# Fused MLP second projection of a two-layer decoder: weight sums by accumulating transfers, with the signs of the seven products turned

## The chip, the cores and the metric

The kernel runs on one core of one Trainium2 chip. The metric is the device time of one execution in microseconds (us). The kernel before takes 1547.85 us (median of 3 runs, 1546.98 to 1550.19).

## The reference: what is computed

Two decoder layers on 512 tokens of width 1024, all in fp32. Each layer has a token mixer, a cross-attention and an MLP, each between two RMS norms. The change lies in the MLP, whose part of the reference is:

```
hdn = jnp.square(jax.nn.relu(rms_norm(x, pre_mlp_g[l]) @ w_up[l]))      # 512 x 4096
x = x + rms_norm(hdn @ w_down[l], post_mlp_g[l])                        # w_down: 4096 x 1024
```

After layer 0's MLP comes the input projection of layer 1's mixer (`w_in`); after layer 1's MLP the result is written out.

## The kernel before, in words

**Products.** An fp32 product is made of three matmuls on halves of the operands: every operand is split into a rounded high part and a rest (`whi`, `wlo` of a weight, `fh`, `fl` of an activation), and `mm` (L239, L240, L241) issues wlo·fh, whi·fl and whi·fh. TensorE (PE) does these. ScalarE (ACT) makes the high part with a copy (L164 for a weight, L201 for an activation), VectorE (DVE) the rest with a subtraction (L165, L203).

**Weights.** `raw_w` (L157) loads a 512 KB tile of weights (128 partitions x 1024 fp32) on SP's queue into one of 8 `raw` buffers; `parts_w` makes `whi` and `wlo` from it, which have 5 buffers each.

**The MLP.** The 4096 hidden features are taken in four chunks of 1024 (`qd_` = 0 to 3), a chunk in two groups g of 512. Per group, an up projection (PE, tiles `pfm`) is evicted by ACT (L1067 relu, L1068 square) into `ra` and `rb`; then `left_forms` makes the seven left operands out of the four quarters a11, a21 (of `ra`) and a12, a22 (of `rb`). After both groups, the second projection is done with seven products in place of eight: p = 1 to 7, each a sum of quarters of the hidden values times a sum of quarters of `w_down`. The four quarters of the weights of each group, b11, b12, b21, b22, are loaded into four `raw` tiles (`B`), and `right_form` turns them into the sum that product p needs by subtractions on DVE, 128 x 1024 each, in place (L1033, L1035, L1037, L1039), before `parts_w`. A product is 24 matmuls of 512 columns (two groups, two row tiles i, two token tiles j, three each). Its result in PSUM (`wa`, `wc`, `we`) is added into the accumulators `acc` in SBUF by DVE (L1105 for the first, L1107 for the others). In chunks 0 to 2 the products come in the order 1, 5, 6, 2, 7, 3, 4; in the last chunk of a layer in the order 1, 2, 5, 6, 3, 7, 4, so that token tiles finish one after the other; `done` then weighs each half by the gain (L1045), `add_post_norm` computes the norm (a power on GpSimd, POOL, L139) and adds to `xs` (L423), and in layer 0 `norm_x` makes the next layer's normed input `xn` on POOL (L408), which PE transposes (L224, `tp`).

**The order of the work.** The program is written in dependency order and a scheduler lays the instructions of each engine in a row; each engine then runs its row in order, and waits where an operand or a buffer isn't ready. POOL has no transfers before the change: its row holds the norms' powers, the `xn` and softmax work.

The program text of the functions that the change touches:

Of the kernel before, what the change touches and what calls it, by code (L numbers as in the profile page):

```python
# [16 lines left out]
OP = mybir.AluOpType  # L17
# [28 lines left out]
def block_kernel(ctx: ExitStack, tc, x, mem, positions, rel_bias, w_in, q_norm_g, w_uq, kv_norm_g,  # L46
# [3 lines left out]
    nc = tc.nc  # L50
# [13 lines left out]
    def unit(name, shape=(128, 512), dt=F32):  # L64
        return un.tile(list(shape), dt, tag="u", name=name)

    def small(name, w):
        return sm.tile([128, 4], F32, tag="sm", name=name)[:, :w]

    def mm_ps(name):  # L70
        return psm.tile([128, 512], F32, tag="mm", name=name)
# [79 lines left out]
    def raw_w(src, r0, kts, c0, width):  # L151
        raw = wp.tile([128, 2, 512], F32, tag="raw", name="raw", bufs=8)

        first = {3: 1, 4: 3}.get(loads[1])
        loads[1] += 1
        with nullcontext() if first is None else tc.issue_after(x_loads[first]):
            loads[2] = nc.sync.dma_start(raw[:, :kts, :width], src[r0:r0 + kts * 128, c0:c0 + width].rearrange(  # L157
                "(k p) c -> p k c", p=128)).ins
        return raw

    def parts_w(raw):
        hi = wp.tile([128, 2, 512], WD, tag="hi", name="whi")
        lo = wp.tile([128, 2, 512], WD, tag="lo", name="wlo")
        nc.scalar.activation(hi, raw, AF.Copy)  # L164
        nc.vector.tensor_sub(lo, raw, hi.bitcast(F32))  # L165
        return hi, lo
# [33 lines left out]
    def split_from(hi, lo, src):  # L200
        token_parts[:] = [nc.scalar.activation(hi, src, AF.Copy).ins]  # L201
        if SPLIT:
            nc.vector.tensor_sub(lo, src, hi.bitcast(F32))  # L203
# [10 lines left out]
    def flush():  # L214
        while late and late[0][0] <= clk[0]:
            late.pop(0)[2]()
# [149 lines left out]
    def feat_major(*a, **k):  # L366
        run(feat_major_steps(*a, **k))
# [44 lines left out]
    def new_xt():  # L412
        h = xtp.tile([128, NK, S], WD, tag="xt", name="xth")
        l = xtp.tile([128, NK, S], WD, tag="xt", name="xtl") if SPLIT else None
        return h, l
# [11 lines left out]
    def row_bcast(src, l):  # L427
        gb = [unit("gb") for _ in range(2)]
        for n in range(2):
            nc.sync.dma_start(gb[n], bass.AP(tensor=src.tensor, offset=src.offset + l * D + n * 512,  # L430
                                               ap=[[0, 128], [1, 512]]))
        return gb
# [129 lines left out]
    for l in range(DEPTH):  # L562
# [434 lines left out]

        acc = [[None, None] for _ in range(NT)]  # L1000
        ss = [small("mss", 2) for _ in range(NT)]
        nxh = nxl = None
# [2 lines left out]
        def left_forms(F, ra, rb):  # L1005

            a11, a21 = ra[:, :, 0:256], ra[:, :, 256:512]
            a12, a22 = rb[:, :, 0:256], rb[:, :, 256:512]

            def part(p, src):  # L1010
                h, lo = unit("fh", (128, 2, 256), WD), unit("fl", (128, 2, 256), WD)
                split_from(h, lo, src)
                F[p].append((h, lo))

            s1, s2 = unit("s1", (128, 2, 256)), unit("s2", (128, 2, 256))
            part(1, a11)
            nc.vector.tensor_add(s1, a21, a22)
            part(5, s1)
            nc.vector.tensor_sub(s2, s1, a11)
            part(6, s2)  # L1020
            part(2, a12)
            nc.vector.tensor_sub(a21, a11, a21)
            part(7, a21)
            nc.vector.tensor_sub(a12, a12, s2)
            part(3, a12)
            part(4, a22)

        def right_form(p, b):


            b11, b12, b21, b22 = b
            if p == 5:
                nc.vector.tensor_sub(b11, b12, b11)  # L1033
            elif p == 6:
                nc.vector.tensor_sub(b11, b22, b11)  # L1035
            elif p == 7:
                nc.vector.tensor_sub(b12, b22, b12)  # L1037
            elif p == 4:
                nc.vector.tensor_sub(b11, b21, b11)  # L1039
            return parts_w({1: b11, 5: b11, 6: b11, 2: b21, 7: b12, 3: b22, 4: b11}[p])  # L1040

        def done(t, n):

# [12 lines left out]
        for qd_ in range(4):  # L1056
            if qd_ == 3 and l < DEPTH - 1:
                nxh, nxl = new_xt()
            F = {p: [] for p in range(1, 8)}
            for g in range(2):  # L1060
                ra = pp.tile([128, 1280], F32, tag="P", name="ra", bufs=2)[:, 0:1024]
                rb = pp.tile([128, 1280], F32, tag="PT", name="rb", bufs=2)[:, 0:1024]
                ra, rb = [r.rearrange("p (k c) -> p k c", k=2) for r in (ra, rb)]

                def ev_up(m, ps, ra=ra, rb=rb):
                    r = (ra, rb)[m // 2][:, m % 2, :]
                    nc.scalar.activation(r, ps, AF.Relu)  # L1067
                    nc.scalar.activation(r, r, AF.Square)  # L1068

                feat_major(w_up[l], (qd_ * 2 + g) * 512, 4, NK, G_MLP + 8 * l, xh_f, xl_f, S, ev_up,  # L1070
                           whole=2 if qd_ == 0 and g == 0 else 0)
                left_forms(F, ra, rb)
            B = [[raw_w(w_down[l], qd_ * 1024 + g * 512 + r * 256, 2, n * 512, 512)
                  for r in range(2) for n in range(2)] for g in range(2)]
            A = [pss.tile([128, 512], F32, tag="s", name="wa") for _ in range(2)]
            C = [pst.tile([128, 512], F32, tag="t", name="wc") for _ in range(2)]
            E = [None] * 2
            end = qd_ == 3


            plan = ((1, A, True, False, ((0, 0),)), (5, C, True, False, ((2, 1),)),
                    (6, A, False, False, ((0, 1),)), (2, E, True, True, ((0, 0),)),
                    (7, A, False, False, ((2, 1),)), (3, C, False, True, ((0, 1),)),
                    (4, A, False, True, ((2, 0),)))
            if end:
                plan = ((1, A, True, False, ((0, 0),)), (2, E, True, True, ((0, 0),)),
                        (5, C, True, False, ((2, 1),)), (6, A, False, False, ((0, 1),)),
                        (3, C, False, True, ((0, 1),)), (7, A, False, True, ((2, 1), (2, 0))),
                        (4, E, True, True, ((2, 0),)))
            for p, ps, first, last, dsts in plan:  # L1090
                if ps is E:
                    E[:] = [mm_ps("we") for _ in range(2)]

                def product(g, i, j, w):
                    c = slice(j * 128, (j + 1) * 128)
                    fh, fl = F[p][g]
                    mm(ps[j], fh[:, i, c], fl[:, i, c], w[0][:, i, :], w[1][:, i, :],
                       first and g + i == 0, g + i == 2, not first)

                def finish(j):  # L1100
                    for d, n in dsts:
                        t = d + j
                        if acc[t][n] is None:
                            acc[t][n] = unit("acc")
                            nc.vector.tensor_copy(acc[t][n], ps[j])  # L1105
                        else:
                            nc.vector.tensor_add(acc[t][n], ps[j], acc[t][n])  # L1107
                        if end and p in (2, 3, 4) or end and p == 7 and n == 1:
                            done(t, n)

                if end and p == 4:
                    for j in range(2):
                        for g in range(2):
                            for i in range(2):
                                product(g, i, j, last_w[g])
                        finish(j)
                        flush()
                    continue
                for g in range(2):
                    w = right_form(p, B[g])  # L1120
                    for i in range(2):
                        for j in range(2):
                            product(g, i, j, w)
                if end and p == 7:
                    last_w = [right_form(4, B[g]) for g in range(2)]
                if end and p == 1:
                    gb = row_bcast(post_mlp_g, l)
                for j in range(2):
                    finish(j)
                if end and p in (2, 5):  # L1130
                    for t in ((0, 1) if p == 2 else (2, 3)):
                        load_x(t, xmid)
                flush()
# [37 lines left out]
```

## Time and profile before

| | before |
|---|---|
| median of 3 runs | 1547.85 us |
| the profiled execution | 1551.81 us |
| span of its instructions | 1550.0 us |
| PE busy | 1509.1 us (97%) |
| DVE busy | 995.9 us (64%) |
| ACT busy | 820.0 us (53%) |
| POOL busy | 239.0 us (15%) |
| transfers | 164.09 MB, 106 GB/s on the mean |

Of the profiled execution's 1551.81 us, 1.81 lie around the span; it stands 3.96 us (0.26%) above the median. A timeline row gives a start, a duration, the engine, the program's line and the tiles; a bracket at its end says how long the engine stood idle before it and what ended the idle time. Busy times of matmuls overlap, so their pace is read from the distance of their starts.

### The profile page before, as it was taken

Reading aid. Unit: us, or ns where it says so; the run is one execution under the profiler, and the core shown is the slowest. Engines: PE = TensorE matmul, PEld = TensorE weight load, DVE = VectorE, ACT = ScalarE, POOL = GpSimd, SP = SyncE. Lnnn points to the kernel's source line nnn. Section 1 sums busy time; section 2 is a strip of 40 time slices with the busy share of each in tenths; the row PEclk is TensorE's granted clock in tenths of the full one; section 3 lists DMA queues with packets and bytes.
Section 4 is the critical chain, followed back from the end, with each engine's and each line's share of the span. In section 5 each row is a group of like instructions: output and inputs, shape, how many; then the busy total and the mean of one; then the engine's idle time right before and its main releaser. Section 6 shows DMA issues by size and latency. Waiting matters only on the chain.

```text
span 1550.0 us, 21290 instructions
## 1 busy us (share of the span) xinstructions
PE 1509.1 (97%) x7861; PEld 1265.6 (82%) x7861; DVE 995.9 (64%) x1780; ACT 820.0 (53%) x1578; POOL 239.0 (15%) x429
## 2 busy tenths in 40 slices
PE   8999999999999999999989999999999999999996
PEld 7777788898898888888868877978988988888885
DVE  5555775456458668585974667664654594958678
ACT  5355666346346464545554566653553654646363
POOL 2133631021020000000011355201111100000000
PEclk9989999999999999999999999999999999999999
DMA  6432223613131505151541322244322324060612
GB/s 235 143 116 69 79 65 109 204 55 119 53 114 50 181 28 177 41 166 59 179 131 51 122 81 91 69 140 145 109 82 68 115 71 155 17 195 20 190 55 82
DMA packets 87404, 164.09 MB, mean 106 GB/s; under 512 B 6230, under 2 KB 12036, under 8 KB 87300
## 3 DMA queue, kind: packets, MB, share of 16 engines
q1 hardware_dynamic: 86724, 161.68, 32.4%
q8 instruction: 62, 1.02, 0.3%
q10 hardware_dynamic: 576, 1.05, 0.2%
q14 instruction: 42, 0.34, 0.1%
HBM read 154.29 MB, written 11.03 MB: 107 GB/s over the span
## 4 chain that ended last, share of the span: by engine, by line
PE 84%; DVE 7%; issue 3%; ACT 2%; DMA 2%; POOL 1%; SPq 0%; DVEq 0%; POOLq 0%; ACTq 0%
PE pfm L240 12%; PE pfm L239 12%; PE pfm L241 12%; PE ptm L239 6%; PE ptm L240 6%; PE ptm L241 6%; PE wa L239 3%; PE wa L240 3%; PE wa L241 3%; PE sp L467 3%; PE op L230 3%; DVE wlo L197 2%; PE ptp L224 2%; PE wc L240 2%; PE wc L239 2%
## 5 line engine op out<-in xcount | busy, mean ns | idle before, releaser
L240 PE MATMUL pfm<-xth,wlo 128*128 128x512 f32 (+1 forms) x896 | 322.4, 360 | 0.6
L239 PE MATMUL pfm<-xtl,whi 128*128 128x512 f32 (+1 forms) x896 | 322.2, 360 | 0.0
L241 PE MATMUL pfm<-xth,whi 128*128 128x512 f32 (+1 forms) x896 | 321.6, 359 | 0.0
L197 DVE SCALAR_TENSOR_TENSOR wlo<-raw,gT,whi 128x512 fp32r<-128x512 f32 (+3 forms) x332 | 229.1, 729 | 131.6 <-ACT whi L192 129.9
L192 ACT ACTIVATE whi<-raw,gT 128x512 fp32r<-128x512 f32 (+2 forms) x324 | 209.2, 697 | 180.3 <-PE pfm L241 87.3
L164 ACT ACTIVATE whi<-raw 128x1024 fp32r<-128x1024 f32 x112 | 118.1, 1060 | 142.9 <-PE pfm L241 52.8
L240 PEld LDWEIGHTS pfm<-xth,wlo 128*128 128x128 f32 x896 | 169.2, 189 | 26.8 <-DVE wlo L197 1.4
L241 PEld LDWEIGHTS pfm<-xth,whi 128*128 128x128 f32 x896 | 169.2, 189 | 25.6 <-issue 0.5
L239 PEld LDWEIGHTS pfm<-xtl,whi 128*128 128x128 f32 x896 | 169.2, 189 | 24.8
L165 DVE TENSOR_TENSOR wlo<-raw,whi 128x1024 fp32r<-128x1024 f32 x112 | 134.8, 1217 | 34.3 <-ACT whi L164 34.3
L139 POOL TENSOR_TENSOR pnr<-pnm,mhalf 128x1 f32<-128x1 f32 x24 | 18.0, 750 | 828.8 <-DVE pnm L420 828.8
L475 POOL TENSOR_SCALAR P<-P,rs 128x128 f32<-128x128 f32 (+3 forms) x128 | 71.5, 563 | 151.6 <-DVE rs L474 81.2
L239 PE MATMUL wa<-wlo,fh 128*128 128x512 f32 x240 | 93.6, 390 | 0.5 <-DVE acc L1105 0.5
L241 PE MATMUL wa<-whi,fh 128*128 128x512 f32 x240 | 93.4, 389 | 0.0
L240 PE MATMUL wa<-whi,fl 128*128 128x512 f32 x240 | 93.4, 389 | 0.0
L473 ACT ACTIVATE P<-P,nm 128x128 f32<-128x128 f32 (+3 forms) x128 | 71.2, 557 | 34.1 <-DVE nm L471 33.4
L185 DVE TENSOR_TENSOR wlo<-raw,whi 128x1024 fp32r<-128x1024 f32 x32 | 39.1, 1222 | 59.3 <-ACT whi L184 58.6
L239 PE MATMUL ptm<-wlo,xth 128*128 128x512 f32 (+2 forms) x192 | 68.6, 359 | 3.4 <-DVE wlo L197 2.5
L184 ACT ACTIVATE whi<-raw 128x1024 fp32r<-128x1024 f32 x32 | 33.9, 1061 | 67.3 <-PE ptm L241 60.2
L240 PE MATMUL ptm<-whi,xtl 128*128 128x512 f32 (+2 forms) x192 | 67.1, 349 | 0.6 <-DVE xtl L203 0.6
L241 PE MATMUL ptm<-whi,xth 128*128 128x512 f32 (+2 forms) x192 | 66.3, 346 | 0.0
L224 PE MATMUL ptp<-ident,P 128*128 128x128 f32 x320 | 50.5, 282 | 3.9 <-ACT PT L494 2.3
(249 smaller groups left out, 3280.4 us busy)
## 6 DMA issues: line engine op xcount, KB each, us to landing
raw<-in_w_up SPq DMA_DIRECT2D x64, 512.0 KB, 4.6
raw<-in_w_down SPq DMA_DIRECT2D x64, 512.0 KB, 4.3
raw<-in_w_in SPq DMA_DIRECT2D x24, 512.0 KB, 5.5
raw<-in_w_xk SPq DMA_DIRECT2D x16, 512.0 KB, 5.4
raw<-in_w_xv SPq DMA_DIRECT2D x16, 512.0 KB, 3.6
raw<-in_w_mix_out SPq DMA_DIRECT2D x16, 512.0 KB, 4.7
raw<-in_w_xq SPq DMA_DIRECT2D x16, 512.0 KB, 6.4
raw<-in_w_xo SPq DMA_DIRECT2D x16, 512.0 KB, 4.1
```

Source lines behind the costliest of these rows:

```text
L164: nc.scalar.activation(hi, raw, AF.Copy)
L165: nc.vector.tensor_sub(lo, raw, hi.bitcast(F32))
L192: weight_parts[:] = [nc.scalar.activation(cols(hi, k, False), cols(raw, k, True), AF.Copy, scale=g).ins]
L197: nc.vector.scalar_tensor_tensor(lv, rv, g, hv, op0=OP.mult, op1=OP.subtract)
L224: ins = nc.tensor.transpose(out_, in_, ident_)
L230: nc.tensor.matmul(ps, lhsT=lhsT, rhs=rhs, start=start, stop=stop)
L239: nc.tensor.matmul(ps, lhsT=lh, rhs=rl, start=first, stop=False, skip_group_check=more)
L240: nc.tensor.matmul(ps, lhsT=ll, rhs=rh, start=False, stop=False, skip_group_check=more)
L241: nc.tensor.matmul(ps, lhsT=lh, rhs=rh, start=False, stop=last, skip_group_check=more)
L467: nc.tensor.matmul(sp[:, :L], lhsT=q[:, i * 128:(i + 1) * 128], rhs=k[:, :L], start=n == 0, stop=n == len(parts) - 1)
L473: nc.scalar.activation(Pi, Pi, AF.Exp, bias=nm[:, i:i + 1], scale=-1.0, accum_out=rs[:, i:i + 1])
L475: nc.gpsimd.tensor_scalar(Pi, Pi, rs[:, i:i + 1], 1.0, op0=OP.mult, op1=OP.mult)
```

## The change

Three things change in the MLP of both layers.

1. The sums of weights are made by a transfer: `right_form` no longer subtracts on DVE, but issues on POOL a `dma_start` with `accum_op=add` that reads another quarter of `w_down` from HBM (512 KB) and adds it into the `raw` tile that is to become the sum. There are 8 of these per chunk (products 5, 6, 7 and 4, two groups), 64 in all. b11 becomes b11+b12 for product 5, then b11+b12+b22 for 6, then that plus b21 for 4; b12 becomes b12+b22 for 7.
2. So that all sums are plain, signs move to the left operands (two `tensor_sub` become `scalar_tensor_tensor`, 128x512) and to the accumulators (a half n=1 is subtracted, and its first write is a multiplication by -1 in place of a copy).
3. Since b12, b21 and b22 are no longer read for sums, their `raw` buffers come free after their own split, and the scheduler lays several rows in another order.

```
-            nc.vector.tensor_add(s1, a21, a22)
+            nc.vector.tensor_sub(s1, a22, a21)
             part(5, s1)
-            nc.vector.tensor_sub(s2, s1, a11)
+            nc.vector.scalar_tensor_tensor(s2, s1, -1.0, a11, op0=OP.mult, op1=OP.subtract)
...
-            nc.vector.tensor_sub(a12, a12, s2)
+            nc.vector.scalar_tensor_tensor(a12, a12, -1.0, s2, op0=OP.mult, op1=OP.subtract)
...
+        def quarter(c, g, r, n):
+
+            r0 = c * 1024 + g * 512 + r * 256
+            return r0, n * 512
+
-        def right_form(p, b):
+        def right_form(p, b, c, g):
             b11, b12, b21, b22 = b
-            if p == 5:
-                nc.vector.tensor_sub(b11, b12, b11)
-            elif p == 6:
-                nc.vector.tensor_sub(b11, b22, b11)
-            elif p == 7:
-                nc.vector.tensor_sub(b12, b22, b12)
-            elif p == 4:
-                nc.vector.tensor_sub(b11, b21, b11)
-            return parts_w({1: b11, 5: b11, 6: b11, 2: b21, 7: b12, 3: b22, 4: b11}[p])
+            tile_, more = {1: (b11, None), 5: (b11, (0, 1)), 6: (b11, (1, 1)), 4: (b11, (1, 0)), 2: (b21, None),
+                           7: (b12, (1, 1)), 3: (b22, None)}[p]
+            if more:
+                r0, c0 = quarter(c, g, *more)
+                nc.gpsimd.dma_start(tile_, w_down[l][r0:r0 + 256, c0:c0 + 512].rearrange("(k p) c -> p k c", p=128),
+                                    accum_op=OP.add)
+            return parts_w(tile_)
...
-                            nc.vector.tensor_copy(acc[t][n], ps[j])
+                            nc.vector.tensor_scalar(acc[t][n], ps[j], (1.0, -1.0)[n], None, op0=OP.mult)
+                        elif n:
+                            nc.vector.tensor_sub(acc[t][n], acc[t][n], ps[j])
```

**POOL, the start of layer 0's MLP.** The pre-MLP norm of the last token tile (`pnr_4613`, `n3r_4624`, `xn_4626`) stands last of the norms; `raw_5114` is b12 of group 0 of chunk 0. Before:

```order
L408 TENSOR_SCALAR xn_4562<-xs_3061,n3r_4560 128x512
L408 TENSOR_SCALAR xn_4564<-xs_3063,n3r_4560 128x512
L139 TENSOR_TENSOR pnr_4613<-pnm_4611,mhalf_105 128x1
L139 TENSOR_TENSOR n3r_4624<-n3m_4622,mhalf_105 128x1
L408 TENSOR_SCALAR xn_4626<-xs_3065,n3r_4624 128x512
```

With the change:

```order
L408 TENSOR_SCALAR xn_4562<-xs_3061,n3r_4560 128x512
L408 TENSOR_SCALAR xn_4564<-xs_3063,n3r_4560 128x512
L1042 DMA raw_5114<-in_w_down 128x2x512
L139 TENSOR_TENSOR pnr_4613<-pnm_4611,mhalf_105 128x1
L139 TENSOR_TENSOR n3r_4624<-n3m_4622,mhalf_105 128x1
L408 TENSOR_SCALAR xn_4626<-xs_3065,n3r_4624 128x512
L408 TENSOR_SCALAR xn_4628<-xs_3067,n3r_4624 128x512
L1042 DMA raw_5122<-in_w_down 128x2x512
L1042 DMA raw_5112<-in_w_down 128x2x512
```

The first accumulating transfer has moved ahead of the norm of the last token tile; all others of the layer come behind it. The same stands in layer 1.

**ACT, the last chunk of layer 1.** `raw_14051` and `raw_14059` are b11 of group 0 and of group 1, `rb_13876` and `ra_13875` the hidden values of group 1, so `fh_14033` is the left operand of product 2, group 1. Before:

```order
L164 ACTIVATE whi_14160<-raw_14051 128x1024
L1068 ACTIVATE rb_13876<-rb_13876 128x512
L164 ACTIVATE whi_14177<-raw_14059 128x1024
L201 ACTIVATE fh_14024<-s1_14017 128x512
L164 ACTIVATE whi_14204<-raw_14051 128x1024
L201 ACTIVATE fh_14029<-s2_14018 128x512
L201 ACTIVATE fh_14033<-rb_13876 128x512
L201 ACTIVATE fh_14038<-ra_13875 128x512
L201 ACTIVATE fh_14043<-rb_13876 128x512
L201 ACTIVATE fh_14047<-rb_13876 128x512
L164 ACTIVATE whi_14221<-raw_14059 128x1024
```

With the change:

```order
L164 ACTIVATE whi_14160<-raw_14051 128x1024
L1072 ACTIVATE rb_13876<-rb_13876 128x512
L164 ACTIVATE whi_14177<-raw_14059 128x1024
L201 ACTIVATE fh_14024<-s1_14017 128x512
L164 ACTIVATE whi_14204<-raw_14051 128x1024
L201 ACTIVATE fh_14029<-s2_14018 128x512
L164 ACTIVATE whi_14221<-raw_14059 128x1024
L201 ACTIVATE fh_14033<-rb_13876 128x512
L201 ACTIVATE fh_14038<-ra_13875 128x512
L164 ACTIVATE whi_14239<-raw_14057 128x1024
```

`whi_14204` and `whi_14221`, the weights of product 6 of both groups, now each come behind an accumulating transfer, and the second has moved ahead of `fh_14033`. The last chunk of layer 0 reads alike. On PE, product 2 of group 1, which reads `fh_14033` and `fh_14038`, stands behind eleven matmuls of product 5 (`wc`) in the new order, and behind one before; DVE's new order has two operations of the left forms between the rests of `whi_14160` and `whi_14177`.

**PE, the end of layer 0.** `we_7307` is the last product of the MLP, `tp_7359` the transposition of token tile 2's `xn` for layer 1, and `ptm` layer 1's input projection, with `wlo_7415`, `wlo_7423` and `wlo_7431` parts of `w_in`. Before, behind `we_7307`:

```order
L224 MATMUL tp_7359<-ident_95,xn_7248 128x128 x4
L224 MATMUL tp_7366<-ident_95,xn_7250 128x128 x4
L239 MATMUL ptm_7444<-wlo_7415,xth_6628 128x512
L240 MATMUL ptm_7444<-whi_7414,xtl_6629 128x512
L241 MATMUL ptm_7444<-whi_7414,xth_6628 128x512
L239 MATMUL ptm_7485<-wlo_7415,xth_6628 128x512
```

With the change, behind `we_7307`:

```order
L239 MATMUL ptm_7444<-wlo_7415,xth_6628 128x512
L240 MATMUL ptm_7444<-whi_7414,xtl_6629 128x512
L241 MATMUL ptm_7444<-whi_7414,xth_6628 128x512
L224 MATMUL tp_7359<-ident_95,xn_7248 128x128 x4
L224 MATMUL tp_7366<-ident_95,xn_7250 128x128 x4
L239 MATMUL ptm_7444<-wlo_7415,xth_6628 128x512
L240 MATMUL ptm_7444<-whi_7414,xtl_6629 128x512
L241 MATMUL ptm_7444<-whi_7414,xth_6628 128x512
L239 MATMUL ptm_7444<-wlo_7423,xth_6628 128x512
L240 MATMUL ptm_7444<-whi_7422,xtl_6629 128x512
L241 MATMUL ptm_7444<-whi_7422,xth_6628 128x512
L239 MATMUL ptm_7444<-wlo_7431,xth_6628 128x512
```

Three matmuls of layer 1 stand ahead of the transposition, and behind it the further `w_in` tiles are used at once, on token tiles that are ready.

## Rows read from the trace of the kernel before

**Rows 1.** The page, busy time of each engine (share of the span, instructions).

```profile
PE 1509.1 (97%) x7861; PEld 1265.6 (82%) x7861; DVE 995.9 (64%) x1780; ACT 820.0 (53%) x1578; POOL 239.0 (15%) x429
```

**Rows 2.** Busy time by stretch: us, PE, PEld, DVE, ACT, POOL, PEclk, DMA share, GB/s.

```profile
455.00:740.00 285.00, 284.74 (x1316) 238.09 (x1315) 198.47 (x251) 150.29 (x218) 0.00 (x0) 1.00 0.31 97
785.00:800.00 15.00, 14.94 (x67) 12.25 (x68) 11.55 (x21) 6.58 (x14) 4.52 (x5) 0.89 0.69 203
1526.00:1550.00 24.00, 12.11 (x53) 9.37 (x51) 18.00 (x29) 6.16 (x14) 3.87 (x4) 0.86 0.24 88
```

**Rows 3.** Groups of DVE by line and form: busy us, mean ns of one.

```profile
L197 DVE SCALAR_TENSOR_TENSOR wlo<-raw,gT,whi 128x512 fp32r<-128x512 f32 x272 | 197.7, 763 | 120.2 <-ACT whi L192 118.6
...
L1035 DVE TENSOR_TENSOR raw<-raw 128x1024 f32<-128x1024 f32 x16 | 19.5, 1219 | 0.2
...
L1019 DVE TENSOR_TENSOR s<-s,ra 128x512 f32<-128x512 f32 x16 | 10.9, 683 | 0.0
```

**Rows 4.** The page, transfers: q1 by packets, MB, share; `w_down` loads, us to landing.

```profile
q1 hardware_dynamic: 86724, 161.68, 32.4%
...
raw<-in_w_down SPq DMA_DIRECT2D x64, 512.0 KB, 4.3
```

**Rows 5.** Timeline of SP's queue, POOL and PE at the start of layer 0's MLP.

```profile
443.39 5.50 SPq L157 DMA_DIRECT2D raw<-in_w_down  x3
...
447.91 0.99 POOL L139 TENSOR_TENSOR pnr<-pnm,mhalf 128x1 f32<-128x1 f32 x1 [1.95 <-DVE pnm L420]
...
452.79 1.39 POOL L408 TENSOR_SCALAR xn<-xs,n3r 128x512 f32<-128x512 f32 x2
...
453.92 1.04 PE L224 MATMUL tp<-ident,xn 128*128 128x128 f32 x8
```

**Rows 6.** Timeline of ACT, DVE and PE in the last chunk of layer 1.

```profile
1502.18 1.06 ACT L164 ACTIVATE whi<-raw 128x1024 fp32r<-128x1024 f32 x1 [0.41 <-PE wa L241]
...
1506.39 0.62 ACT L201 ACTIVATE fh<-rb 128x512 fp32r<-128x512 f32 x1
1506.91 0.62 ACT L201 ACTIVATE fh<-ra 128x512 fp32r<-128x512 f32 x1
...
1501.29 1.23 DVE L165 TENSOR_TENSOR wlo<-raw,whi 128x1024 fp32r<-128x1024 f32 x1 [1.90 <-ACT whi L164]
1502.43 0.68 DVE L1017 TENSOR_TENSOR s<-ra,rb 128x512 f32<-128x512 f32 x1
...
1499.26 0.39 PE L239 MATMUL wa<-wlo,fh 128*128 128x512 f32 x1
...
1507.42 0.39 PE L239 MATMUL wc<-wlo,fh 128*128 128x512 f32 x1
```

**Rows 7.** Timeline of DVE and PE in chunk 1 of layer 0.

```profile
569.68 1.23 DVE L165 TENSOR_TENSOR wlo<-raw,whi 128x1024 fp32r<-128x1024 f32 x1 [0.40 <-ACT whi L164]
...
582.21 0.39 PE L240 MATMUL wc<-whi,fl 128*128 128x512 f32 x1
```

**Rows 8.** Timeline of DVE and PE at the end of layer 0.

```profile
767.14 1.22 DVE L1039 TENSOR_TENSOR raw<-raw 128x1024 f32<-128x1024 f32 x1
...
779.12 1.09 PE L224 MATMUL tp<-ident,xn 128*128 128x128 f32 x8 [2.37 <-POOL xn L408]
...
785.07 0.50 PE L239 MATMUL ptm<-wlo,xth 128*128 128x512 f32 x1 [2.01 <-DVE wlo L197]
785.40 0.59 PE L240 MATMUL ptm<-whi,xtl 128*128 128x512 f32 x1
```

**Rows 9.** Timeline of DVE, POOL and PE at the end of layer 1.

```profile
1531.92 1.22 DVE L1039 TENSOR_TENSOR raw<-raw 128x1024 f32<-128x1024 f32 x1
...
1534.91 1.22 DVE L165 TENSOR_TENSOR wlo<-raw,whi 128x1024 fp32r<-128x1024 f32 x1
...
1545.06 1.42 DVE L423 SCALAR_TENSOR_TENSOR xs<-acc,pnr,xs 128x512 f32<-128x512 f32 x2 [0.67 <-POOL pnr L139]
...
1532.08 1.47 POOL pnr L139
...
1536.18 0.50 PE L239 MATMUL we<-wlo,fh 128*128 128x512 f32 x1 [1.09 <-DVE wlo L165]
```

More of the change, by code (lines that the diff above doesn't have):

```diff
@@ L1072, in block_kernel @@
                 left_forms(F, ra, rb)
-            B = [[raw_w(w_down[l], qd_ * 1024 + g * 512 + r * 256, 2, n * 512, 512)
-                  for r in range(2) for n in range(2)] for g in range(2)]
+            B = [[raw_w(w_down[l], quarter(qd_, g, r, n)[0], 2, n * 512, 512) for r in range(2) for n in range(2)] for g in range(2)]
             A = [pss.tile([128, 512], F32, tag="s", name="wa") for _ in range(2)]
@@ L1119, in block_kernel @@
                 for g in range(2):
-                    w = right_form(p, B[g])
+                    w = right_form(p, B[g], qd_, g)
                     for i in range(2):
@@ L1124, in block_kernel @@
                 if end and p == 7:
-                    last_w = [right_form(4, B[g]) for g in range(2)]
+                    last_w = [right_form(4, B[g], qd_, g) for g in range(2)]
                 if end and p == 1:
```

## The prediction

> **What bounds the kernel now.** First the page's busy times: PE is busy in 97% of the span, DVE in 64%, POOL in 15% [rows 1]. Then the same by stretch, since shares over the whole span hide what ends last in a stage. In the MLP of layer 0, from 455 to 740 us, PE is busy in 284.74 of 285 us and DVE in 198.47 [rows 2]: whatever DVE is relieved of there lies beside PE and is worth nothing. PE stands idle only where the norms close a layer: it is busy in 12.11 of the last 24 us, and around 779 us it waits 2.37 and 2.01 us [rows 2, 8]. So the question is not how much DVE work goes, but what happens at a few places: the two ends, where DVE's queue is the chain, and the starts and last chunks, where the new transfers stand in somebody's way.
>
> **What goes and comes.** Removed are four lines of subtractions, each 16 times some 1.22 us as L1035 is [rows 3]: 64 x 1.22 = 78 us of DVE. Added on DVE: 32 `scalar_tensor_tensor` in place of subtractions; the nearest row is 763 ns against 683 [rows 3], so 32 x 0.08 = 2.6 us, under PE. The turned signs of the accumulators keep operations of the same size. Added on POOL are 64 transfers of 512 KB, 33.6 MB. q1 moved 161.68 MB in 32.4% of 1550 us, or 322 GB/s while busy [rows 4]; the new bytes would take 104 us at that rate, 7% of the span, on engines that are free in 69% of a typical MLP stretch [rows 2]. Bytes are no bound. Latency may be.
>
> **The price that the trace doesn't show.** Call L the time from when an accumulating transfer may be issued to when its sum can be read. POOL issues none before. The lower bound is the plain load of the same size, 4.3 us [rows 4]. An addition must fetch the tile as well as the weights: one more pass of 512 KB at 322 GB/s is 1.6 us. And POOL has to issue it, where its own small operations hold it for 0.99 to 1.47 us when DVE works beside them [rows 5, 9]. I take 4.3 + 1.6 + 1.0 = 6.9 us, the middle one since each part has a row near it. The upper bound is two loads one after the other with SP's 5.50 us for three issues [rows 5] as price of an issue: 2 x 4.3 + 1.8 = 10.4 us.
>
> The Trainium skill, "DMA: Bandwidth & Descriptors", section on the anatomy of one DMA, gives 2.0 us plus the bytes at 436 GB/s for a transfer issued by GpSimd, an estimate of 3.2 us for these, which is below what plain loads need here. By that price the sum below would be about -5 us.
>
> **Chunks 0 to 2: nothing.** The rest of product 5's weights is done on DVE at 569.68 + 1.23 = 570.9, which lets product 6's transfer go; at 582.21 PE reads the rest of the left operand that ACT and DVE make just behind those weights [rows 7]. ACT's copy of the weights (0.97 us from start to start), its copy of the operand (0.52) and DVE's rest (0.68) lie between: 570.9 + L + 2.2 must be at most 582.2, so L may reach 9.1 us. Above that every one of the six chunks pays L - 9.
>
> **Start of an MLP, twice.** The first accumulating transfer now stands ahead of the last token tile's norm on POOL, and waits for the load of b12. SP issues the three loads from 443.39 [rows 5]; with 4.3 us b12 lands at about 447.7. The norm's power started at 447.91 before, and the transposition on PE at 453.92 follows `xn` (452.79 + 0.70, two in 1.39) without slack [rows 5]. If POOL is held for 1.0 us by the issue, the power starts at 448.7: +0.8 us, bounds 0 and 1.6 (an issue of 1.8). Twice, layer 1 taken as equal: **+1.6 us** (0 to 3.2).
>
> **Last chunk, twice.** Here ACT's new order puts product 6's second weight copy ahead of product 2's left operands. In layer 1 DVE ends the rest of group 0 at 1502.43; two left-form operations of 0.60 us (from start to start) and the rest of group 1 of 1.22 follow, up to 1504.85, when the second transfer may go [rows 6]. Then L, ACT's copy (0.97) and two operand copies (0.52 + 0.62) [rows 6]: `fh_14038` is ready at 1506.95 + L. PE's pace is 36 matmuls in 1507.42 - 1499.26 = 8.16 us, or 0.227 each [rows 6]; eleven more bring it to 1509.9, where it needs that operand. The stall is L - 3.0 us: with 6.9 it is 3.9, with 4.3 it is 1.3, with 10.4 it is 7.4. DVE stands behind the same copies, but with no one else waiting for it longer than PE does. Two layers: **+7.8 us** (2.6 to 14.8).
>
> **End of layer 0.** Two subtractions of 1.22 us (one at 767.14) leave DVE's row between the norms of token tiles 0 to 2, and `w_in` is loaded earlier since the buffers of b21 and b22 come free. PE's losses there are 2.37 + 2.01 us of waits [rows 8] and, at a granted clock of 0.89 over 15 us, 1.65 us more [rows 2]: 6.0 in all. The first wait hangs on the norm chain and loses up to 2.4; the second is for a weight that now comes earlier, and three matmuls (0.7 us) now fill the first. I take two thirds: **-4.0 us** (-6 to -1).
>
> **Final tail.** The last subtraction at 1531.92 and the one before it stand between the norms; product 4's weights wait for them, up to 1534.91 + 1.22, and PE with them (1.09 us at 1536.18) [rows 9]. Following DVE's new row with these durations, the last `xs` starts 2.1 us before its 1545.06: less than 2.44, for POOL's powers stay in the chain. **-2.1 us** (-3 to -1).
>
> **Sum.** 1.6 + 7.8 - 4.0 - 2.1 = **+3.3 us**. The profiled execution, 1550.0 of span and 1.81 around it, would become 1555.1; it stood 3.96 above the median, so against the median of 1547.85 I forecast **1551.2 us**, +0.21%. From no change, 0.2% (3.1 us) is about what a measurement of this kernel can tell.
>
> **Rivals.** (1) The accumulating transfer is cheap: faster. If L is no more than a plain load, 4.3 us, and POOL is free at once, the starts cost 0 and the last chunks 2.6; with the two ends 2.6 - 6.1 = -3.5, or 1544.4. It decides below L of about 4.5 us. For it: a load of the same bytes lands in 4.3 [rows 4], and the transfer engines are idle in the last chunk. Against it: the second stream and POOL's issue. The skill's 3.2 us speak for it; no run here shows them. Chance 0.22.
> (2) It is dear: with L = 10.4, +14.8 in the last chunks, +3.2 at the starts, and 6 x (10.4 - 9) = 8.4 in chunks 0 to 2, less 6.1: +20.3, or 1568. For it: POOL's operations are held by DVE's, 1.47 against 0.99 us [rows 5, 9], and DVE is busy in 18 of the last 24 us [rows 2]; a held issue lengthens L wherever DVE works. Chance 0.12. The skill's "SBUF — State Buffer", section on who interferes with whom, says that descriptors written by GpSimd starve while DVE runs its two-port modes, but counts `tensor_tensor`, which is most of DVE's work here, as not doing that; no run here shows either.
> (3) The transfer is as I cost it, but the stall is hidden or the ends give more, and nothing can be told: L of 5.5 gives 5.0 in the last chunks, 1.6 at the starts and -6.1, so +0.5, or 1548.4. Chance 0.32, with all cases within 3.1 us.
> The forecast itself, slower by 3 to 15 us with a stall in each last chunk, has 0.34, which also covers a smaller gain at the ends (-2 in place of -6.1 makes +7.4).
>
> **How the numbers follow.** Slower by over 0.2%: 0.34 + 0.12 = 0.46; within: 0.32; faster: 0.22. The range reaches from the cheap case, 1544, to L of about 9 with half the gain at the ends (12 + 3 - 3 = +12, so 1560, and 1561 for a clock lost after a stall as in [rows 2]); beyond lie the dear case and a faster one than 1544, together under 0.2.
>
> **What would show it.** DVE's busy time falls by about 75 us and the middle of the MLPs stays at a PE that is always busy: right, and worth nothing. A queue of POOL with 64 transfers, landing in 6 to 7 us. PE waiting some 4 us for an operand of ACT's about 10.5 us after the last chunk of each layer begins, and none in chunks 0 to 2. The transposition at the MLP's start late by 1 us. The waits at 779 and 785 shrunk, and product 4's wait gone. The forecast is wrong if transfers land in under 4.5 us, if they take over 9, or if PE has no wait in the last chunks because something else reaches them later.

## The result and the profile after

The changed kernel takes 1561.16 us (median of 5 runs, 1554.63 to 1562.36) against 1547.85 before. These two medians lie 13.3 us apart (a ratio of 1.0086); the ratio on record, which is not formed from the two medians, is 1.0064, with a 95% interval of 1.0042 to 1.0086, or some 9.9 us slower. That one is used below. The forecast was +3.3 us, with a range up to 1561: the sign was right, the size too small.

Lines of the page of the changed kernel, to set beside [rows 1, 4]: the span, busy times, the new queue, POOL's new group, and the landing times (issue to landing, median us) of loads on SP's queue and of accumulating transfers on POOL's.

```profile
span 1559.7 us, 21452 instructions
...
PE 1512.7 (97%) x7861; PEld 1267.8 (81%) x7861; DVE 929.5 (60%) x1716; ACT 820.5 (53%) x1578; POOL 312.9 (20%) x493
...
q0 software_dynamic: 17408, 33.56, 13.2%
...
L1042 POOL DMA_DIRECT2D raw<-in_w_down x64 | 77.2, 1206 | 531.6 <-DMA raw<-in_w_down 189.5
...
raw<-in_w_down SPq DMA_DIRECT2D x64, 512.0 KB, 4.5
raw<-in_w_down POOLq DMA_DIRECT2D x64, 512.0 KB, 6.0
```

DVE gave up 66 us of busy time (summed over its instructions, which overlap, the 75 of the forecast) and the program became longer: nearly all of what was removed was not on the path. An accumulating transfer costs POOL 1.206 us to issue and lands 6.0 us after the issue begins, where the same bytes on SP's queue land in 4.5.

The start of layer 0's MLP (POOL, then PE), to set beside [rows 5]:

```profile
447.72 1.38 POOL L1042 DMA_DIRECT2D raw<-in_w_down  x1 [1.86 <-ACT whi L192]
448.69 1.01 POOL L139 TENSOR_TENSOR pnr<-pnm,mhalf 128x1 f32<-128x1 f32 x1
...
454.34 1.33 PE L224 MATMUL tp<-ident,xn 128*128 128x128 f32 x8 [0.35 <-POOL xn L408]
```

The same stretches as in [rows 2] (us, PE, PEld, DVE, ACT, POOL, PEclk, DMA share, GB/s), the middle of layer 0's MLP and the end of layer 0:

```profile
455.00:740.00 285.00, 284.14 (x1314) 237.60 (x1315) 168.48 (x222) 149.45 (x216) 32.46 (x27) 1.00 0.63 151
785.00:800.00 15.00, 13.75 (x70) 11.08 (x71) 13.07 (x24) 9.63 (x24) 4.62 (x6) 1.00 0.48 152
```

In the middle, DVE is busy 30 us less, PE 0.6 us less, and the share of the transfer engines has doubled from 0.31 to 0.63, though they move only half as much again (151 GB/s against 97). At 785 us the granted clock is 1.00 where it was 0.89.

What PE waited for at the end of layer 0 (735 to 800 us), then in the last chunk and tail of layer 1 (1480 to 1560): us in total, times, longest.

```profile
PE tp L224 <- POOL xn L408: 3.3, 3, 1.3
PE we L239 <- ACT fh L201: 3.2, 1, 3.2
PE ptm L240 <- DVE xtl L203: 0.6, 1, 0.6
...
PE we L239 <- ACT fh L201: 6.2, 1, 6.2
```

The two waits for ACT's `fh` are the new ones, one in each last chunk. Product 4's wait of 1.09 us [rows 9] and the wait of 2.01 us for a weight of layer 1 [rows 8] are gone. The timeline of the last chunk of layer 1 (POOL, ACT, then PE), to set beside [rows 6]:

```profile
1507.19 1.20 POOL L1042 DMA_DIRECT2D raw<-in_w_down  x1 [15.75 <-DVE s L1018]
1508.98 1.20 POOL L1042 DMA_DIRECT2D raw<-in_w_down  x1 [0.59 <-DVE wlo L165]
...
1512.82 1.06 ACT L164 ACTIVATE whi<-raw 128x1024 fp32r<-128x1024 f32 x1 [5.33 <-DMA raw<-in_w_down]
...
1518.31 1.06 ACT L164 ACTIVATE whi<-raw 128x1024 fp32r<-128x1024 f32 x1 [3.92 <-DMA raw<-in_w_down]
1519.28 0.61 ACT L201 ACTIVATE fh<-rb 128x512 fp32r<-128x512 f32 x1
...
1519.94 1.22 PE L239 MATMUL we<-wlo,fh 128*128 128x512 f32 x2 [6.16 <-ACT fh L201]
1520.96 0.63 PE L241 MATMUL wc<-whi,fh 128*128 128x512 f32 x1
...
1525.65 0.41 PE L239 MATMUL we<-wlo,fh 128*128 128x512 f32 x1
```

The chain can be read downward: POOL issues product 6's second transfer at 1508.98; ACT, in order, stands until it has landed and copies the weights at 1518.31; only then comes the operand of product 2, which needed no transfer at all, at 1519.28; PE starts on it at 1519.94. After the wait eleven matmuls from 1520.96 to 1525.65 take 4.69 us, 0.426 each against 0.227 before, 11 x 0.20 = 2.2 us more. The stretch behind this wait, and the one behind the wait of 3.2 us in layer 0, by the same columns as above:

```profile
1520.00:1525.60 5.60, 5.60 (x13) 4.39 (x14) 4.26 (x6) 2.51 (x4) 1.21 (x1) 0.50 0.69 132
752.00:757.00 5.00, 4.61 (x20) 3.81 (x21) 5.00 (x7) 3.73 (x6) 1.21 (x1) 1.00 0.83 133
```

The granted clock was 0.50, the lower of the two levels (1.2 of 2.4 GHz), after 6.16 us without a matmul, and 1.00 after 3.19 us. The length of the wait alone does not decide it, as the last section shows.

Product 6's second transfer in layer 1 landed 9.2 us after its issue, beside other loads (xs_later, below, tests what they cost). SP's row for the residual's loads, and the middle of the chunk by the columns above, before; then the row with the change:

```profile
1504.89 8.86 SPq L87 DMA_DIRECT2D xs<-xmid  x8
...
1504.00:1510.00 6.00, 5.98 (x27) 4.63 (x26) 6.00 (x10) 2.63 (x4) 0.00 (x0) 1.00 0.56 188
```

```profile
1508.60 14.30 SPq L87 DMA_DIRECT2D xs<-xmid  x7
```

In layer 0 the changed kernel issues these loads only from 757.65 on, when product 6's transfers have landed: SP stands at loads of `w_in` until 756. Before the change they went out from 742.66 on.

**A ledger by stretches.** The stages outside the MLP differ between executions though their work is the same (layer 0's MLP started between 440.6 and 448.1 us in the profiles below), so kernels are compared by stretches between events on PE's timeline: the MLP's start (transposition of token tile 2 to that of tile 3), the chunks (from there to product 1 of the last chunk), layer 0's end (from there to the first `pfm` matmul of layer 1's input stage), and layer 1's last chunk with the tail (from product 1 to the end of the span).

| us | start, layers 0 and 1 | chunks, layers 0 and 1 | end of layer 0 | last chunk and tail, layer 1 | sum against before | ratio of times [95%] |
|---|---|---|---|---|---|---|
| before | 7.03, 7.03 | 283.10, 283.14 | 72.02 | 50.74 | 0 | 1 |
| changed kernel | 7.54, 7.32 | 284.04, 284.10 | 72.07 | 56.73 | +8.7 | 1.0064 [1.0042, 1.0086] |
| signs_only | 7.03, 7.02 | 283.15, 283.12 | 71.99 | 50.67 | -0.1 | 1.0002 [0.9990, 1.0014] |
| last6_dve | 7.36, 7.29 | 283.62, 284.58 | 67.54 | 48.17 | -4.5 | 0.9970 [0.9958, 0.9982] |
| operand_first | 7.36, 7.30 | 283.93, 283.77 | 70.06 | 50.39 | -0.3 | 0.9998 [0.9987, 1.0009] |
| plain_load | 7.32, 7.29 | 282.86, 282.86 | 67.88 | 54.20 | -0.7 | 0.9996 [0.9982, 1.0009] |
| xs_later | 7.33, 7.30 | 283.67, 283.86 | 71.48 | 55.74 | +6.3 | 1.0069 [1.0046, 1.0092] |
| last_p47 | 7.02, 7.03 | 283.12, 283.15 | 67.58 | 49.09 | -6.1 | 0.9959 [0.9946, 0.9972] |
| last_p4 | 7.02, 7.01 | 283.13, 283.16 | 67.55 | 48.94 | -6.3 | 0.9956 [0.9941, 0.9970] |
| last_p4_again | 7.03, 7.02 | 283.13, 283.13 | 67.52 | 49.22 | -6.0 | 0.9960 [0.9947, 0.9974] |
| early_dve4 | 7.03, 7.02 | 283.15, 283.16 | 70.27 | 51.91 | -0.5 | 0.9998 [0.9984, 1.0013] |
| mid_dve4 | 7.04, 7.02 | 283.11, 283.11 | 72.91 | 50.69 | +0.8 | 1.0000 [0.9986, 1.0013] |

The sums, of one profile each, stand close to the ratios throughout (0.1% is 1.5 us) except for xs_later, which was timed only twice; so the stretches hold the effect. Each edit also lets the scheduler lay its rows anew, so a run can differ from the changed kernel in more than the lines shown.

### The profile page after: what moved, and what is told of

It is laid out like the page before. It is cut to its first block, busy times and chain, and to the rows that moved or that the text cites. A ratio compares the mean times of both kernels' runs of the same rounds, so it can differ in the third digit from the quotient of the medians.

```text
span 1559.7 us, 21452 instructions
## 1 busy us (share of the span) xinstructions
PE 1512.7 (97%) x7861; PEld 1267.8 (81%) x7861; DVE 929.5 (60%) x1716; ACT 820.5 (53%) x1578; POOL 312.9 (20%) x493
## 3 DMA queue, kind: packets, MB, share of 16 engines
q0 software_dynamic: 17408, 33.56, 13.2%
## 4 chain that ended last, share of the span: by engine, by line
PE 74%; DVE 8%; issue 6%; DMA 5%; ACT 4%; POOL 1%; SPq 0%; DVEq 0%; POOLq 0%; ACTq 0%
PE pfm L240 10%; PE pfm L239 10%; PE pfm L241 10%; PE ptm L239 6%; PE ptm L240 6%; PE ptm L241 6%; DMA raw<-in_w_down 3%; PE sp L467 3%; PE op L230 3%; PE wa L239 3%; PE wa L241 3%; PE wa L240 3%; PE ptp L224 2%; DVE wlo L197 2%; ACT whi L192 2%
## 5 line engine op out<-in xcount | busy, mean ns | idle before, releaser
L1042 POOL DMA_DIRECT2D raw<-in_w_down x64 | 77.2, 1206 | 531.6 <-DMA raw<-in_w_down 189.5
```

The lines of the kernel that those rows point to most:

```text
L1042: nc.gpsimd.dma_start(tile_, w_down[l][r0:r0 + 256, c0:c0 + 512].rearrange("(k p) c -> p k c", p=128), accum_op=OP.add)
```

## The experiments

**signs_only** undoes the transfers and keeps the signs.

```
-            if more:
+            if more and (True):
+                nc.vector.tensor_add(tile_, tile_, b[more[0] * 2 + more[1]])
+            elif more:
```

> The turned signs with every sum of weights made by DVE again, no accumulating transfer. Theory: the signs cost nothing and the gains at the two ends belong to DVE's relief, so it takes the time of the kernel before within 0.1% and shows its waits at the ends (2.4 and 2.0 us at the end of layer 0, 1.1 us at product 4). Rival: the signs and the new order they bring cost or gain by themselves, over 2 us either way.

The ratio was 1.0002, and its waits on PE are those of before:

```profile
PE tp L224 <- POOL xn L408: 2.4, 1, 2.4
PE ptm L239 <- DVE wlo L197: 2.0, 1, 2.0
...
PE we L239 <- DVE wlo L165: 1.1, 1, 1.1
```

The signs are free to within the interval, 0.9990 to 1.0014, and everything else belongs to the transfers and to what they move.

**last6_dve** gives product 6 of the last chunks (4 of 64 sums) back to DVE.

```
-            if more:
+            if more and (c == 3 and p == 6):
+                nc.vector.tensor_add(tile_, tile_, b[more[0] * 2 + more[1]])
+            elif more:
```

> As the changed kernel, but in the last chunk of each layer the weights of product 6 are added by DVE again; 60 of the 64 accumulating transfers stay. Theory: nearly all of the loss is the two waits for product 6's transfer, 3.2 us in layer 0 and 6.2 us plus some 2.6 us of lower clock in layer 1, in front of product 2's operand. Then the waits vanish, and what is left against the kernel before is +0.4 and +0.3 at the starts, about +0.9 in chunks 0 to 2 of each layer, -2.1 at the end of layer 0 and -2.6 at the end: -2 us, about 1546. Rival: the transfers slow the rest through shared transfer engines or POOL holding DVE; then it stays 5 us or more above the kernel before.

The ratio fell from 1.0064 to 0.9970: faster than the kernel before. What PE waits for at the end of layer 0:

```profile
PE tp L224 <- POOL xn L408: 2.5, 2, 1.4
PE ptm L240 <- DVE xtl L203: 0.3, 1, 0.3
```

From 1480 us on it waits for nothing that the view names. The other 60 transfers cost 0.6 us at the starts and 2.0 in the chunks (0.5 in layer 0, 1.4 in layer 1), and the two ends give 4.5 and 2.6. The rival, that 60 transfers as such slow the rest by 5 us, falls.

**operand_first** keeps all 64 transfers and puts ACT's copy of product 2's operand ahead of product 6's weights.

(`tc.issue_after` makes what is issued under it stand behind the named instruction in its engine's row.)

```
...
             part(2, a12)
+            after2[:] = [token_parts[0]]
...
-            return parts_w(tile_)
+            with tc.issue_after(after2[0]) if c == 3 and p == 6 else nullcontext():
+                return parts_w(tile_)
```

> As the changed kernel with all 64 accumulating transfers, but in the last chunk ACT copies product 2's left operand of group 1 ahead of product 6's weights. Theory that the order on ACT turns the landing into a wait: the landing stays 5.5 to 9.2 us, PE's waits of 3.2 and 6.2 us vanish, since product 6's weights are needed only 16 to 19 us after the chunk's start; about 1546 to 1548. Rival that the latency itself is the cost: the wait moves to product 6 (PE wait at wa of 2 to 5 us in one or both layers), 1551 to 1556.

ACT's row in layer 1's last chunk, and PE's waits from 1480 us on:

```profile
1500.10 0.61 ACT L201 ACTIVATE fh<-rb 128x512 fp32r<-128x512 f32 x1
1502.77 1.06 ACT L164 ACTIVATE whi<-raw 128x1024 fp32r<-128x1024 f32 x1 [2.06 <-DMA raw<-in_w_down]
...
1507.42 1.06 ACT L164 ACTIVATE whi<-raw 128x1024 fp32r<-128x1024 f32 x1 [3.07 <-DMA raw<-in_w_down]
...
PE wa L239 <- DVE wlo L165: 0.4, 1, 0.4
```

ACT still stands for both landings, but the operand is through at 1500.10 and PE waits 0.4 us in place of 6.2. So it was the order on ACT that made a wait of a landing; the rival (the wait moves to product 6) shows with 0.3 and 0.4 us only. It doesn't reach the 1546 to 1548 hoped for (1548.93, the time of before): the tail from the last matmul on is 11.41 us, 1.4 longer than last6_dve's 10.01, and the end of layer 0 gains 2.0 where that gains 4.5. Why the ends gain less in this order was not tried.

**plain_load** leaves out `accum_op=OP.add` and nothing else; its products are other ones, so only its time is of use.

> The changed kernel with the addition left out: the same 64 transfers on POOL's queue overwrite the tile in place of adding to it, so products 5, 6, 7 and 4 use a plain quarter of the weights. Theory that the add's second stream is paid for: median landing falls from 6.0 us to 4.3 to 4.6 us as for plain loads on SP's queue, and the waits in the last chunks shrink by about 1.5 us each. Rival that the price lies in POOL's issue: landing stays near 6.0 us.

Queue, POOL's group and landing of this kernel:

```profile
q0 software_dynamic: 9216, 33.56, 6.4%
...
L1042 POOL DMA_DIRECT2D raw<-in_w_down x64 | 46.6, 728 | 552.6 <-DMA raw<-in_w_down 267.0
...
raw<-in_w_down POOLq DMA_DIRECT2D x64, 512.0 KB, 4.1
```

Without the addition the same bytes land in 4.1 us, and POOL's issue takes 0.728 us. The addition costs 6.0 - 4.1 = 1.9 us of latency, of which 0.48 lie in POOL's issue; the packets go from 9216 to 17408 and the share of the transfer engines doubles, 6.4% to 13.2%, for the same 33.56 MB. The waits in the last chunks shrink by 2.3 and 2.4 us, to 0.9 and 3.8, where 1.5 us each were expected, and the chunks are 1.2 us shorter than in the changed kernel, and 0.2 to 0.3 shorter than before.

The Trainium skill, "DMA: Bandwidth & Descriptors", section on the anatomy of one DMA, has the formula from which the prediction's estimate of 3.2 us for such a transfer comes. The runs show 4.1 us without and 6.0 us with the addition; the measurement decides. The Trainium skill, "SBUF — State Buffer", section on who interferes with whom, says that GpSimd can be kept from writing descriptors while DVE runs a two-port mode. POOL's 64 issues took 1.194 to 1.381 us in the changed kernel, so no run here shows it.

**xs_later** holds back the residual's loads in layer 1, which SP issued from 1508.60 on, in the middle of product 6's transfers.

```
...
-                if end and p in (2, 5):
+                if end and p in (2, 5) and l < DEPTH - 1:
...
+                if end and p == 6 and l == DEPTH - 1:
+                    with tc.issue_after(token_parts[0]):
+                        for t in range(4):
+                            load_x(t, xmid, nc.scalar)
```

> The changed kernel, but in layer 1 the eight loads of the residual (256 KB each) are issued by ACT behind product 6's weights in place of SP as soon as buffers are free. Theory that the long landing in layer 1 is shared bandwidth with these loads: product 6's second transfer lands in 5.5 to 6.5 us in place of 9.2, PE's wait at product 2 in layer 1 falls from 6.2 to some 3 us, as in layer 0. Rival that two accumulating transfers 1.8 us apart slow each other: landing stays at 8 us or more.

Landing times of the `raw` tile's transfers from POOL in layer 1's last chunk, min, median and max, of the changed kernel and then of this one, and this one's wait:

```profile
DMA to landing us min/median/max: 5.5/7.0/9.2
```

```profile
DMA to landing us min/median/max: 5.9/5.9/6.6
...
1515.73 1.22 PE L239 MATMUL we<-wlo,fh 128*128 128x512 f32 x2 [3.56 <-ACT fh L201]
1516.75 0.63 PE L241 MATMUL wc<-whi,fh 128*128 128x512 f32 x1
```

The longest landing falls from 9.2 to 6.6 and the wait from 6.16 to 3.56, both by 2.6 us: this part of the wait came from the residual's loads, of which five of eight (1.25 MB) were issued while the transfer was under way; between 1508.60 and 1518.30 the transfer engines were busy throughout (a share of 1.00, at 228 GB/s). The stretch from product 1 up to the last matmul fell by as much (47.00 to 44.43), but the rest of the ledger's column, from there to the end, grew from 9.73 to 11.31, so nothing was won in time: ACT's next copy of weights now waits 3.42 us behind the issues, and a rest of product 4's weights stands between the norms on DVE again, at 1540.30, as before the change [rows 9]. The lower clock came after this wait of 3.56 us too (0.63 us in the row at 1516.75; 0.50 granted from 1515.7 to 1521.0).

**last_p47 and last_p4** keep transfers only for products 7 and 4, or 4 alone, of the last chunks.

(The edit of last_p4; last_p47 has `p in (4, 7)`.)

```
-            if more:
+            if more and (not (c == 3 and p == 4)):
+                nc.vector.tensor_add(tile_, tile_, b[more[0] * 2 + more[1]])
+            elif more:
```

> Accumulating transfers only for products 7 and 4 of the last chunk of each layer (8 of 64); all other sums on DVE as before, signs turned. Theory: DVE's relief inside chunks 0 to 2 is worth nothing, and the transfers there cost 0.3 us at each start and 0.5 to 1.4 us per layer in the chunks; the gains belong to product 4's and 7's sums leaving DVE at the two ends (and to buffers freed there): starts and chunks as before, 4.5 us less at the end of layer 0, 2.6 us less in the last chunk and tail of layer 1, -7 us or a ratio near 0.9955. Rival: the gain at the end of layer 0 needs the emptier DVE of the whole chunk and the earlier free buffers of all sums; then it gains 3 us or less, a ratio of 0.998 or more.

> Accumulating transfers only for product 4 of the last chunk of each layer (4 of 64), all other sums on DVE. Theory that only the two subtractions for product 4, which stand between the norms on DVE, matter: the same gain as with products 7 and 4, ratio 0.995 to 0.9965. Rival that the freed buffers of b22 (read by product 7's sum too) let the next layer's weights in: the gain at the end of layer 0 halves, ratio 0.997 to 0.9985.

Both are the fastest measured, 0.9959 and 0.9956 (last6_dve's interval still overlaps theirs); starts and chunks are as before to 0.03 us. The norms of the first two token tiles in layer 1, before, and then the transfers and these norms in last_p4, read:

```profile
1530.52 1.42 DVE L423 SCALAR_TENSOR_TENSOR xs<-acc,pnr,xs 128x512 f32<-128x512 f32 x2 [0.44 <-POOL pnr L139]
...
1533.58 1.42 DVE L423 SCALAR_TENSOR_TENSOR xs<-acc,pnr,xs 128x512 f32<-128x512 f32 x2 [0.44 <-POOL pnr L139]
```

```profile
1505.57 1.24 POOL L1044 DMA_DIRECT2D raw<-in_w_down  x1 [294.90 <-DVE wlo L165]
1512.53 1.20 POOL L1044 DMA_DIRECT2D raw<-in_w_down  x1 [5.72 <-DVE wlo L165]
...
1524.84 1.42 DVE L423 SCALAR_TENSOR_TENSOR xs<-acc,pnr,xs 128x512 f32<-128x512 f32 x2 [0.46 <-POOL pnr L139]
...
1526.98 1.42 DVE L423 SCALAR_TENSOR_TENSOR xs<-acc,pnr,xs 128x512 f32<-128x512 f32 x2 [0.67 <-POOL pnr L139]
```

The second `xs` pair follows the first by 2.14 us, and by 3.06 before, where, with the subtraction and the weights of product 4 beside the norms, DVE comes to the rest of those weights only at 1534.91 [rows 9]. Four transfers give all of last6_dve's gain at the end of layer 0 (4.5 us) and 1.8 of its 2.6 us in layer 1 (1.7 in last_p47, 1.5 in the repetition); why the tail gains less was not tried. The half gain that the rival foresaw without b22's freed buffers did not appear. But a transfer for product 4 frees b21's buffers too: last_p4 issues two loads of `w_in` from 728.20 on, and the kernel before its first at 758.04. No run separates what that adds.

> The kernel last_p4 once more, beside mid_dve4 on the same chip, so that the two are compared directly: 0.9945 to 0.997 again if its gain is no accident of one chip.

The repetition on another chip, beside mid_dve4, gave 0.9960 [0.9947, 0.9974].

**early_dve4 and mid_dve4** ask whether the transfer is needed at all: no transfers, but product 4's two sums earlier on DVE, behind product 6's weights or behind product 3's (`p == 3` in the line below).

```
-            if more:
+            if more and c == 3 and p == 4:
+                pass
+            elif more:
+                nc.vector.tensor_add(tile_, tile_, b[more[0] * 2 + more[1]])
...
+                if end and p == 6:
+                    for g in range(2):
+                        nc.vector.tensor_add(B[g][0], B[g][0], B[g][2])
```

> No accumulating transfer at all: every sum of weights is made by DVE, but in the last chunk product 4's two sums are written right behind product 6's weights instead of behind product 7's, so that they stand on DVE ahead of the norms of the last token tiles. Theory that the gain comes from where product 4's sums stood on DVE and not from the transfer: the same gain as with four accumulating transfers, ratio 0.995 to 0.997, the wait at product 4 (1.1 us) gone, the end of layer 0 some 4 us shorter. Rival that the transfer itself is needed, because DVE has no room ahead of the norms: DVE's 4.9 us of sums only come earlier and delay product 7's weights, ratio 0.998 to 1.000.

> As early_dve4, no accumulating transfer, but product 4's two sums stand on DVE behind product 3's weights, 2.4 us later in DVE's row, so that product 3 no longer waits for them. Theory that only the place of the two sums on DVE matters: the wait of 2.3 us at product 3 that early_dve4 showed in both layers is gone, the wait at product 4 too, ratio 0.995 to 0.998. Rival that the transfer is needed since DVE has no 2.4 us to spare anywhere between product 6 and the norms: a wait at product 7 or 4 takes its place, and the ratio stays at 0.9985 or more.

Both take the time of before (0.9998 and 1.0000). In early_dve4 the sums stand ahead of product 3's weights on DVE, and PE waits for those:

```profile
1514.36 2.35 DVE L1135 TENSOR_TENSOR raw<-raw 128x1024 f32<-128x1024 f32 x2
...
1519.10 0.79 PE L239 MATMUL wc<-wlo,fh 128*128 128x512 f32 x1 [2.28 <-DVE wlo L165]
1519.69 0.63 PE L240 MATMUL wc<-whi,fl 128*128 128x512 f32 x1
```

Without its wait of 2.28 us there, early_dve4's end of layer 0 would be 4.0 us shorter than before, near the 4.5. That points to DVE's emptier row between the norms as the source of the gain, and to the wait as what the sums cost elsewhere; no run shows it by itself. In mid_dve4 that wait is gone, product 4's is back (1480 us on, near the 1.09 of before), and the wait for `xn` at layer 0's end is 5.7 us, 2.4 before:

```profile
PE we L239 <- DVE wlo L165: 1.0, 2, 0.8
...
PE tp L224 <- POOL xn L408: 5.7, 2, 3.5
```

At these two places DVE has no 2.4 us to spare between product 6 and the norms; other places were not tried. Here the transfer does something that moving the sums did not.

## Why the prediction was right in sign and too small

- **DVE's relief in the chunks is worth nothing:** right for chunks 1 and 2 of each layer, which take 81.60 us in every kernel here. Chunk 0 takes 82.1 to 82.2 us before and 81.60 in plain_load, where nothing waits: there the new rows and the relief are worth 0.5 us, which the landing of the accumulating transfers eats up.
- **Chunks 0 to 2, forecast 0:** wrong, +0.94 and +0.96, in two places. 0.3 of each belongs to the start: behind the event at which the ledger's chunks begin, the second half of `xn` is late as well (the eight transpositions take 1.33 us, and 1.04 before [rows 5]). The other 0.65 is all in chunk 0, where PE waits for DVE to evict the chunk's first results, `wa`; here in layer 0, before and then with the change:

```profile
508.43 0.50 PE L239 MATMUL wa<-wlo,fh 128*128 128x512 f32 x1 [0.26 <-DVE acc L1105]
```

```profile
508.38 0.50 PE L239 MATMUL wa<-wlo,fh 128*128 128x512 f32 x1 [0.85 <-DVE acc L1108]
```

In the new order PE comes to this matmul after 66 matmuls of the chunk in place of 72, or 1.4 us sooner; DVE, behind weights that hang on a transfer, starts to evict `wa` only 0.7 us sooner. In plain_load it does so 2.0 us sooner and PE doesn't wait. The step looked at product 6's operand only, not at the accumulators.
- **The starts, forecast 0.8 each:** right in mechanism; +0.51 and +0.29 in the ledger, 0.8 and 0.6 with what falls behind its event. The norm's power started at 448.69, as forecast. That is luck in part: the profile puts the end of POOL's wait at 447.72 down to a copy of ACT's, not to b12's load. And PE had 0.4 us of slack where the step took none.
- **The last chunks, forecast L - 3.0 with L of 6.9, so 3.9 each:** the mechanism was right at its place, and operand_first and last6_dve show it by taking it away. The term was mis-sized: 3.19 and 6.16 us, 9.35 in place of 7.8. What failed is the single L: in layer 0's last chunk the transfers land in 5.8 to 6.3 us, in layer 1's, beside the residual's loads, in up to 9.2. With these, L - 3.0 gives 3.3 and 6.2. That it fits so well is luck in part: PE needed only the first of the two operands counted (0.5 us less), and the second transfer went out 0.4 us later in the chunk than counted. The loads could have been seen: rival 1 took the transfer engines for idle in the last chunk, but before the change eight loads go out there from 1504.89 on, where the step sends the transfer off at 1504.85, and the engines' share is 0.56. And the 2.2 us of lower clock after the long wait stood in the range but not in the sum.
- **The end of layer 0, forecast -4.0:** right. Take 3.19 from the changed kernel's 72.07 and it is -3.1; without the wait, last6_dve shows -4.5.
- **The tail, forecast -2.1:** right, -2.6 in last6_dve. The changed kernel loses product 4's wait of 1.1 us, and the time behind its last matmul falls by 1.5 (from 11.2 to 9.7).
- **The price of a transfer, 6.9 us as 4.3 + 1.6 + 1.0:** near. The addition measured 1.9 for 1.6, POOL's issue 1.2 for 1.0, but the landing of 6.0 is counted from the issue's start, so the parts overlap. The bound of 10.4 rests on a wrong reading: SP's three issues in 5.50 us [rows 5] take 0.4 us each, and SP waits between them. And the transfers took 13.2% of the transfer engines' span, not the 7% of the forecast, which counted their bytes once; this bounds nothing here.

In the MLP's stretches: +0.8 (starts), +1.9 (chunks), +9.35 (waits) and some 2.2 (clock) less 3.1 and 2.6 at the ends make +8.6, against 8.7 measured there. The 5.3 us above the forecast of +3.3 are 1.6 of longer waits, 2.2 of clock, 1.9 in the chunks and 0.4 less gain at the ends, less 0.8 at the starts.

## What to carry to other kernels

A transfer that takes work off an engine is worth what its place on the path is worth: 60 of 64 relieved an engine that had time, and four, at the two ends, gave most of the gain (0.9956) with none of the cost at the starts, in the chunks and in front of product 2. An engine that runs its row in order, as ACT does here, turns the latency of a transfer into the wait of whatever stands behind it, even of work that needs no transfer (6.16 us against 0.4 in operand_first); so look, for every wait that a change adds, at the next rows of that engine's queue. And price a latency at the place where it is paid: the same transfer took 6 us in one layer and 9 in the other, beside the residual's loads, which the trace of before already showed in that place.

## What the runs showed of the hardware that was not expected

The addition in a transfer doubles its packets (9216 to 17408) and the transfer engines' share (6.4% to 13.2%) at the same bytes moved, and costs POOL 1.206 us to issue in place of 0.728. And PE's waits of 6.16, 3.77 (plain_load, layer 1), 3.56 and 2.28 us (early_dve4, layer 1) were followed by 3 to 6 us at the lower clock, while waits of 3.54 (mid_dve4), 3.19 and again 2.28 us (early_dve4, layer 0) were not. Behind the two waits of 2.28 us, layer 0's and then layer 1's:

```profile
758.40:761.40 3.00, 3.00 (x13) 2.51 (x14) 3.00 (x3) 0.00 (x0) 0.00 (x0) 1.00 0.87 265
1519.10:1522.20 3.10, 3.10 (x7) 2.48 (x8) 3.10 (x3) 0.00 (x0) 0.00 (x0) 0.50 0.00 0
```

So the length of the wait doesn't set them apart; what does was not settled. The 2.2 us of clock in the changed kernel are a reading of one execution.
